# Retention's first rotation behind the value loads, most of y's low parts on GpSimd, and layer 1's low parts one gated block later

## The chip, the cores and the metric

The kernel runs on one core of a Trainium2 chip, as one launch. The metric is the device time of that launch in microseconds (us), lower is better. Five engines work side by side, each through its own list of instructions and in the order of that list: TensorE (PE in the profile: matrix products and transposes, results in banks of PSUM), VectorE (DVE), ScalarE (ACT), GpSimd (POOL) and SyncE (SP), which here does little but start the DMA transfers of the loads and stores. An instruction starts when it is at the head of its engine's list and the semaphores it waits for have come.

## The reference

Two layers on an input of 1024 rows by 1024 columns. Layer 0 projects the normalised input and feeds two branches, an S5 state-space model with a gated linear unit (GLU) and a retention in chunks of 64 rows, each with its gate, and projects both back. Layer 1 is a convolution module. Cut to what the change touches:

```python
# S5 branch, after the scan
y = jax.nn.gelu(y)
y = y * jax.nn.sigmoid(y @ glu_w + glu_b)
# retention: q, k rotated (rope), 8 heads of 64, values 128 wide, 16 chunks of 64 rows
scores = einsum('bnihd,bnjhd->bnhij', qc, kc) * intra
intra_out = einsum('bnhij,bnjhe->bnihe', scores, vc)
kv = einsum('bnjhd,jh,bnjhe->bnhde', kc, k_dec, vc)
_, s_prev = lax.scan(lambda s, kv_n: (chunk_decay * s + kv_n, s), 0, kv)
cross = einsum('bnihd,ih,bnhde->bnihe', qc, q_dec, s_prev)
out = intra_out + cross
out = (out - mean(out)) * rsqrt(var(out) + EPS)          # per head
x = x + concat(y * silu(g_s5), out * silu(g_ret)) @ w_out
# layer 1
a, b, g = split(rmsnorm(x) @ w_in_c, 3)
u = causal_conv31(a * sigmoid(b)) + conv_b
u = silu(layernorm(u)) * silu(g)
x = rmsnorm(x + u @ w_out_c)
```

## The kernel before

**Products.** Everything is held with channels or rows on 128 partitions, in tiles of 128 x 512 (a half of the 1024 rows). To keep float32 accuracy, each operand is split into a high part and a low part: ScalarE casts `f` to `fp32r` (`xh`, `wh`, `yh`), another engine takes the difference (`xl`, `wl`, `yl`), and each block of 128 x 128 x 512 is three matmuls:

```python
nc.tensor.matmul(ps, wh[:, kb, :], xh, start=start, stop=False)
nc.tensor.matmul(ps, wh[:, kb, :], xl, start=False, stop=False)
self.last_mm = nc.tensor.matmul(ps, wl[:, kb, :], xh, start=False, stop=stop)
```

A GLU product is eight such blocks, 24 matmuls, for one half of the rows and 128 columns. Weights come block by block in tiles `wf`, `wh`, `wl` of three buffers each, in the order of a plan (..., V1_0, V1_1, ..., V5_1, k1, q1, k2, ..., glu0, glu1, ...).

**Order.** The program is written as one stream of instructions; a scheduler gives each engine its order by a simulated timeline and by priorities. Inside `with issue_after(x)` an instruction comes no earlier than `x` in that order. The lists that come out are fixed: what stands behind a late instruction on its engine waits with it.

**The values** (`ret_values`). The value projection is made of seven smaller products of sums of blocks (`V_ORDER` 1, 2, 6, 7, 3, 4, 5). `fetch` loads their left operands (`xf30` is block 0 of product 3's operand, here used by product 7), casts (`xh`) and subtracts (`xl`); `scaled` and `summed` add the banks `mm_v` into the value tiles `v`. Between the products `y_pass` loads a part of the S5 output (`yp`), applies gelu on ScalarE and stores it as `yn_d`.

**Retention** works on four pairs of heads. `ret_proj` makes k and q, each times cos and sin (`kcos`, `ksin`), exchanges the sin rows by four DMAs of 128 KB (`kswp<-ksin`), and adds on GpSimd (`krot`, `qrot`). It is a generator; for pair 0 it is run to its end before the values, for the others k's projection comes before the pair ahead and the rest in it. `ret_heads` then runs, per pair: transposes of k (`ktp`, `kt`), `kv`, the 15 state steps `S` one after the other on VectorE, scores `sp` and their mask `sc` (`self.masked`, one per half of the rows), outputs `ro`, statistics (`st`, `mv`, `rs`), normed outputs `on`, transposed back (`rt`) and multiplied into the gate (`grl`).

**Layer 1's low parts.** `weight_low(k)` prepares 32 tiles of layer 1's weights: load `lf`, cast `lh` on ScalarE, subtract, store to DRAM. Tiles 0 to 17 go along with retention's pairs (subtraction on GpSimd), 18 to 31 along with the GLU (on VectorE, two sets of one buffer for each step):

```python
def lows(n):
    for k in islice(left, n):
        self.weight_low(lp, k, (("cs", "pilot"), ("cq", "sq")), 1)
```

**y and the GLU** (`layer0_back_and_layer1`). `load_split` loads y (gelu's output) back in 16 tiles `yf<kb>_<half>`, two to one `wf` buffer, and splits them into `yh`, `yl`. Its order gates, before, are the mask of pair 2 (`self.masked_2`) for the first half, and for the second `self.last_kt` and `self.masked[0]` of pair 3. Each GLU product `mm_glu<nb>_<half>` goes through tanh (`sg`) on ScalarE and `sg = (sg + 1) * yg` on VectorE, where `yg` is the S5 gate times y from GpSimd; for half 0 a split (`ysh`, `ysl`) follows, for half 1 the sums `t3f`, `t2f` that the output projection takes. `lows` is called in both cases.

Of the kernel before, what the change touches and what calls it, by code (L numbers as in the profile page):

```python
# [23 lines left out]
HALF = 512  # L24
# [33 lines left out]
class Trunk:  # L58
# [877 lines left out]
    def retention(self, st):  # L936
        nc, A = self.nc, self.A
        r0 = self.r0 = self.pool("ret0", 1, stack=st)
        early = ExitStack()
        rq = self.rq = self.pool("retq", 1, stack=early, side="right")  # L940
        self.vt = [[(r0 if d else rq).tile([P, 4, HALF], F32, name=f"v{d}_{h}") for h in range(2)] for d in range(2)]
        self.rk = rq.tile([P, 2, T], F32, name="ropek")
        nc.sync.dma_start(self.rk[:], A["rope_k"])
        for i in range(2):
            for c in (slice(0, HALF), slice(HALF, T)):
                nc.gpsimd.tensor_tensor(self.rk[:, i, c], self.rk[:, i, c], self.R[:, c], op=ALU.mult)
        self.mask = r0.tile([P, 4, 64], F32, name="retmask")
        nc.sync.dma_start(self.mask[:], A["ret_mask"])
        self.g64 = r0.tile([P, 4], F32, name="g64")
        nc.sync.dma_start(self.g64[:], A["ret_g64"])  # L950
        self.kdec = r0.tile([P, NH], F32, name="kdec")
        nc.sync.dma_start(self.kdec[:], A["ret_kdec"])
        self.reps = r0.tile([P, NH], F32, name="reteps")
        nc.sync.dma_start(self.reps[:], A["ret_eps"])
        cur = list(self.ret_proj(0))[-1]
        for pair in range(4):
            if pair == 0:
                with ExitStack() as vst:
                    V = self.ret_values(self.pool("vp", 1, stack=vst))
                self.rp = self.pool("ret", 1, stack=st)  # L960
                self.crossed(0)
                ry = self.pool("retl", 1, stack=early, side="right")

            def lows(n, behind):
                with self.tc.issue_after(behind.ins):
                    for k in range(n * LOWS // 6, (n + 1) * LOWS // 6) if pair < 3 else ():
                        self.weight_low(ry, k, (("la", "lb"), ("la", "lb")), 3, nc.gpsimd)

            def turned():
                lows(2 * pair + 1, self.last_kt)  # L970
                if pair == 3:
                    early.close()
                    self.lp = self.pool("l1", side="right")
            lows(2 * pair, self.last_rs if pair else self.last_sum)
            ahead = pair in AHEAD and self.ret_proj(pair + 1)
            if ahead:
                next(ahead)
            cur = self.ret_heads(pair, *cur, V, turned, lambda: list(ahead)[-1] if ahead else None)
            if pair < 3:
                self.crossed(pair + 1)  # L980

    def ret_proj(self, pair):
        nc, A, rp = self.nc, self.A, self.r0
# [14 lines left out]
        def turn(nm):  # L998
            cos, sin = parts[nm]
            swp = self.rq.tile([P, T], F32, name=f"{nm}swp_{pair}", tag="swp", bufs=1)  # L1000
            o = rp.tile([P, T], F32, name=f"{nm}rot_{pair}", tag=f"{nm}rot", bufs=1)
            for b in range(4):
                s = b ^ 1
                nc.sync.dma_start(swp[32 * b:32 * b + 32, :], sin[32 * s:32 * s + 32, :])
            for c in (slice(0, HALF), slice(HALF, T)):
                nc.gpsimd.tensor_tensor(o[:, c], cos[:, c], swp[:, c], op=ALU.add)
            return o


        project("k")  # L1010
        yield None
        krot = turn("k")
        project("q")
        yield krot, turn("q")

    def ret_values(self, vp):
# [4 lines left out]
        def fetch(i, tiles):  # L1021
            for kb, (a, b) in enumerate(tiles):
                g = self.vec(V_NG0, kb)
                f = vp.tile([P, HALF], F32, name=f"xf{i}{kb}", tag="xf", bufs=4)
                nc.sync.dma_start(f[:], self.xt_d[i][kb] if i else self.A["xT"][kb, :, HALF:])
                if i:
                    nc.scalar.copy(a[:], f[:])
                    v.tensor_tensor(b[:], f[:], a[:].bitcast(F32), op=ALU.subtract)
# [177 lines left out]
    def layer0_back_and_layer1(self, st):  # L1206
# [42 lines left out]
        for nb, h in [(nb, h) for nb in range(6) for h in range(2)] + [(6, 0), (7, 0), (6, 1), (7, 1)]:  # L1249
# [12 lines left out]
            if h == 0:  # L1262
                a, b = (self.op_tile(opB, "B0", f"ys{q}{nb}") for q in "hl")
                nc.scalar.mul(a[:], sg[:], 0.5)
                glu_end = v.scalar_tensor_tensor(b[:], sg[:], 0.5, a[:].bitcast(F32), op0=ALU.mult, op1=ALU.subtract)
                ys0[nb], sg0[nb] = (a, b), sg
                lows(2 if nb else 0)
                continue
            yr1 = lp.tile([P, HALF], F32, name=f"yr1_{nb}", tag="tp", bufs=TP)
            nc.sync.dma_start(yr1[:], self.yr_d[rows(nb), hs(1)])  # L1270
            t3f[nb], t2f[nb] = (opB.tile([P, HALF], F32, name=f"{n}_{nb}", tag="B1") for n in ("t3f", "t2f"))
            v.scalar_tensor_tensor(t3f[nb][:], sg[:], -0.5, yr1[:], op0=ALU.mult, op1=ALU.add)
# [508 lines left out]
```

## Time and profile before

| | us |
|---|---|
| median of 3 runs (1184.87, 1189.07, 1189.58) | 1189.07 |
| profiled execution | 1189.67 |
| its span, first to last instruction | 1187.9 |
| busy TensorE | 1159.5 |
| busy VectorE | 906.0 |
| busy GpSimd | 693.9 |
| busy ScalarE | 542.8 |
| mean granted TensorE clock | 0.994 |

A row of a view reads: start and duration in us, engine, line, operation, out<-in by the program's names (with their numbers left out), shapes, how many in a row, and in brackets the idle time of that engine just ahead and what ended it. A row with a bar (|) is a group: busy time in all and mean ns of one, then the idle time before its members. `SPq` is SyncE's queue, busy while a transfer is being issued. `min/median/max` rows are in ns. Line numbers are those of the kernel before.

### The profile page before, as it was taken

How to read it: one execution, taken by the hardware profiler on the slowest of the kernel's cores; microseconds unless marked ns; L12 is line 12 of the kernel's file. 1: busy time of each engine (PE TensorE's matmuls, PEld its weight loads, DVE VectorE, ACT ScalarE, POOL GpSimd, SP SyncE). 2: the span in 40 equal slices, each digit the busy share in tenths (PEclk: the TensorE clock that was granted, in tenths of full speed). 3: DMA queues.
4: the chain of work that ended last, by engine and by line, in shares of the span. 5: the costliest groups of instructions: out<-in, count | busy, mean ns of one | idle time of the engine just before them, and what ended most of it. 6: DMA issues, size and time to landing. Idle time of an engine off the chain costs nothing.

```text
span 1187.9 us, 18547 instructions
## 1 busy us (share of the span) xinstructions
PE 1159.5 (98%) x6662; PEld 962.4 (81%) x6662; DVE 906.0 (76%) x1531; ACT 542.8 (46%) x819; POOL 693.9 (58%) x495
## 2 busy tenths in 40 slices
PE   9999999999999999998899999999999999999997
PEld 7888888888888788886778788778888888888877
DVE  7875789999615577678766887469999999989633
ACT  7212333332226633122543535367755678444662
POOL 2049999888732335452343033428895679977742
PEclk9999999999999999999999999999999999999999
DMA  9353478788888768878986577776448654357863
GB/s 341 107 183 102 140 271 311 267 278 279 268 302 286 254 208 270 231 232 260 348 292 214 156 231 241 271 258 204 169 141 300 231 179 133 121 180 250 271 242 142
DMA packets 135548, 272.17 MB, mean 229 GB/s; under 512 B 13216, under 2 KB 46368, under 8 KB 135328
## 3 DMA queue, kind: packets, MB, share of 16 engines
q1 hardware_dynamic: 134304, 266.80, 67.4%
q10 hardware_dynamic: 1152, 4.19, 0.9%
q8 instruction: 52, 0.85, 0.3%
q14 instruction: 40, 0.33, 0.1%
HBM read 192.89 MB, written 71.76 MB: 223 GB/s over the span
## 4 chain that ended last, share of the span: by engine, by line
PE 82%; DMA 9%; DVE 4%; ACT 1%; POOL 1%; issue 1%; SPq 1%; DVEq 0%; POOLq 0%; ACTq 0%
PE mm_g L277 7%; PE mm_g L278 7%; PE mm_g L276 7%; PE mm_w L278 3%; PE mm_w L276 3%; PE mm_w L277 3%; PE mm_a L278 2%; PE mm_b L277 2%; PE mm_a L277 2%; PE mm_a L276 2%; PE mm_b L278 2%; PE mm_oc L278 2%; PE mm_u L278 2%; PE mm_b L276 2%; PE mm_u L277 2%; PE mm_oc L277 2%
## 5 line engine op out<-in xcount | busy, mean ns | idle before, releaser
L1471 DVE SCALAR_TENSOR_TENSOR cv<-u,convw,cv 128x512 f32<-128x512 f32 x358 | 244.8, 751 | 6.6 <-ACT cv L1457 5.1
L1451 POOL TENSOR_TENSOR tp<-tp,tp 128x512 f32<-128x512 f32 x104 | 138.8, 1337 | 30.7 <-ACT tp L1450 25.4
L278 PE MATMUL mm_g<-xh,wl_g 128*128 128x512 f32 x256 | 100.9, 394 | 0.0
L277 PE MATMUL mm_g<-xl,wh_g 128*128 128x512 f32 x256 | 100.7, 393 | 0.0
L276 PE MATMUL mm_g<-xh,wh_g 128*128 128x512 f32 x256 | 100.6, 393 | 0.0
L1450 ACT ACTIVATE tp<-u,convw 128x512 f32<-128x512 f32 x104 | 69.7, 714 | 11.0 <-POOL tp L1451 10.8
L277 PEld LDWEIGHTS mm_g<-xl,wh_g 128*128 128x128 f32 x256 | 48.1, 188 | 11.2 <-issue 1.6
L278 PEld LDWEIGHTS mm_g<-xh,wl_g 128*128 128x128 f32 x256 | 48.1, 188 | 10.5
L276 PEld LDWEIGHTS mm_g<-xh,wh_g 128*128 128x128 f32 x256 | 48.1, 188 | 9.5
L278 PE MATMUL mm_oc<-zh,wl_woc 128*128 128x512 f32 (+1 forms) x152 | 54.5, 360 | 1.3 <-DMA wl_woc<-lo_woc 1.3
L276 PE MATMUL mm_glu<-yh,wh_glu 128*128 128x512 f32 x128 | 51.1, 399 | 4.6 <-ACT sg L1260 4.1
L276 PE MATMUL mm_oc<-zh,wh_woc 128*128 128x512 f32 (+1 forms) x152 | 54.3, 362 | 0.0
L277 PE MATMUL mm_oc<-zl,wh_woc 128*128 128x512 f32 (+1 forms) x152 | 54.0, 357 | 0.0
L278 PE MATMUL mm_a<-h1h,wl_ca 128*128 128x512 f32 x128 | 50.1, 392 | 1.6 <-DMA wl_ca<-lo_ca 1.6
L277 PE MATMUL mm_u<-xl,wh_u 128*128 128x512 f32 x128 | 50.0, 390 | 0.9 <-DVE xl L390 0.9
L277 PE MATMUL mm_glu<-yl,wh_glu 128*128 128x512 f32 x128 | 50.8, 397 | 0.0
L278 PE MATMUL mm_glu<-yh,wl_glu 128*128 128x512 f32 x128 | 50.5, 394 | 0.0
L276 PE MATMUL mm_g<-h1h,wh_cg 128*128 128x512 f32 x128 | 50.4, 394 | 0.0
L276 PE MATMUL mm_a<-h1h,wh_ca 128*128 128x512 f32 x128 | 50.3, 393 | 0.0
L278 PE MATMUL mm_b<-h1h,wl_cb 128*128 128x512 f32 x128 | 50.3, 393 | 0.0
L278 PE MATMUL mm_g<-h1h,wl_cg 128*128 128x512 f32 x128 | 49.9, 390 | 0.0
L277 PE MATMUL mm_g<-h1l,wh_cg 128*128 128x512 f32 x128 | 49.9, 390 | 0.0
(812 smaller groups left out, 3600.7 us busy)
## 6 DMA issues: line engine op xcount, KB each, us to landing
wf_g<-w_ab SPq DMA_DIRECT2D x16, 512.0 KB, 5.4
a<-w_out SPq DMA_DIRECT2D x32, 256.0 KB, 4.1
ws<-a SPq DMA_DIRECT2D x32, 256.0 KB, 4.7
lf<-w_c SPq DMA_DIRECT2D x32, 256.0 KB, 5.2
wf_p<-ws SPq DMA_DIRECT2D x16, 512.0 KB, 4.1
wf_cb<-w_c SPq DMA_DIRECT2D x16, 512.0 KB, 5.1
wf_ca<-w_c SPq DMA_DIRECT2D x16, 512.0 KB, 4.9
wl_cb<-lo_cb SPq DMA_DIRECT2D x16, 512.0 KB, 3.6
```

The source lines that it names most:

```text
L276: nc.tensor.matmul(ps, wh[:, kb, :], xh, start=start, stop=False)
L277: nc.tensor.matmul(ps, wh[:, kb, :], xl, start=False, stop=False)
L278: self.last_mm = nc.tensor.matmul(ps, wl[:, kb, :], xh, start=False, stop=stop)
L1450: nc.scalar.mul(sk[:], u[:, k:k + HALF], cw[:, nb, k:k + 1])
L1451: gp.tensor_tensor(s0[:], s0[:], sk[:], op=ALU.add)
L1471: v.scalar_tensor_tensor(dst[:], *tap, accs_[i][:], op0=ALU.mult, op1=ALU.add)
```

## The change

Three edits. (1) For pair 0, k and q are projected first, and the exchanges and additions of both come behind the values: the generator is started ahead of `ret_values` and finished after it, and the exchanges carry the gate `issue_after(self.fetched)`, the last load of `fetch`. For the other pairs the gate is that same load, long past. (2) In `load_split`, y's first half and the even tiles of the second go to GpSimd without a gate; the odd tiles of the second stay on VectorE, gated as before. (3) `lows` in the GLU starts one block later in both places: from block 2 on. There are still 14 tiles, and as many matmuls.

```diff
@@ -952,12 +952,14 @@
         nc.sync.dma_start(self.kdec[:], A["ret_kdec"])
         self.reps = r0.tile([P, NH], F32, name="reteps")
         nc.sync.dma_start(self.reps[:], A["ret_eps"])
-        cur = list(self.ret_proj(0))[-1]
+        first = self.ret_proj(0)
+        next(first)
         for pair in range(4):
             if pair == 0:
                 with ExitStack() as vst:
                     V = self.ret_values(self.pool("vp", 1, stack=vst))
                 self.rp = self.pool("ret", 1, stack=st)
+                cur = list(first)[-1]
                 self.crossed(0)
                 ry = self.pool("retl", 1, stack=early, side="right")
 
@@ -999,18 +1001,24 @@
             cos, sin = parts[nm]
             swp = self.rq.tile([P, T], F32, name=f"{nm}swp_{pair}", tag="swp", bufs=1)
             o = rp.tile([P, T], F32, name=f"{nm}rot_{pair}", tag=f"{nm}rot", bufs=1)
-            for b in range(4):
-                s = b ^ 1
-                nc.sync.dma_start(swp[32 * b:32 * b + 32, :], sin[32 * s:32 * s + 32, :])
+            with self.tc.issue_after(self.fetched.ins):
+                for b in range(4):
+                    s = b ^ 1
+                    nc.sync.dma_start(swp[32 * b:32 * b + 32, :], sin[32 * s:32 * s + 32, :])
             for c in (slice(0, HALF), slice(HALF, T)):
                 nc.gpsimd.tensor_tensor(o[:, c], cos[:, c], swp[:, c], op=ALU.add)
             return o
 
 
         project("k")
-        yield None
-        krot = turn("k")
-        project("q")
+        if pair:
+            yield None
+            krot = turn("k")
+            project("q")
+        else:
+            project("q")
+            yield None
+            krot = turn("k")
         yield krot, turn("q")
 
     def ret_values(self, vp):
@@ -1022,7 +1030,7 @@
             for kb, (a, b) in enumerate(tiles):
                 g = self.vec(V_NG0, kb)
                 f = vp.tile([P, HALF], F32, name=f"xf{i}{kb}", tag="xf", bufs=4)
-                nc.sync.dma_start(f[:], self.xt_d[i][kb] if i else self.A["xT"][kb, :, HALF:])
+                self.fetched = nc.sync.dma_start(f[:], self.xt_d[i][kb] if i else self.A["xT"][kb, :, HALF:])
                 if i:
                     nc.scalar.copy(a[:], f[:])
                     v.tensor_tensor(b[:], f[:], a[:].bitcast(F32), op=ALU.subtract)
@@ -1218,7 +1226,12 @@
 
             def put(kb, h, f):
                 a, b = (self.op_tile(self.opA, f"A{h}", f"{name}{q}{kb}_{h}") for q in "hl")
-                self.split(f, a, b, v, None if halves else self.masked_2 if h == 0 else self.last_kt if kb < 6 else self.masked[0])
+                if halves:
+                    self.split(f, a, b, v)
+                elif h == 0 or kb % 2 == 0:
+                    self.split(f, a, b, gp)
+                else:
+                    self.split(f, a, b, v, self.last_kt if kb < 6 else self.masked[0])
                 res[h].append((a, b))
             for h in range(2):
                 for kb in range(KB):
@@ -1264,14 +1277,14 @@
                 nc.scalar.mul(a[:], sg[:], 0.5)
                 glu_end = v.scalar_tensor_tensor(b[:], sg[:], 0.5, a[:].bitcast(F32), op0=ALU.mult, op1=ALU.subtract)
                 ys0[nb], sg0[nb] = (a, b), sg
-                lows(2 if nb else 0)
+                lows(2 if nb > 1 else 0)
                 continue
             yr1 = lp.tile([P, HALF], F32, name=f"yr1_{nb}", tag="tp", bufs=TP)
             nc.sync.dma_start(yr1[:], self.yr_d[rows(nb), hs(1)])
             t3f[nb], t2f[nb] = (opB.tile([P, HALF], F32, name=f"{n}_{nb}", tag="B1") for n in ("t3f", "t2f"))
             v.scalar_tensor_tensor(t3f[nb][:], sg[:], -0.5, yr1[:], op0=ALU.mult, op1=ALU.add)
             glu_end = v.scalar_tensor_tensor(t2f[nb][:], sg0.pop(nb)[:], 0.5, t3f[nb][:], op0=ALU.mult, op1=ALU.add)
-            lows(1 if 0 < nb < 6 else 0)
+            lows(1 if 1 < nb < 6 else 0)
 
         def operand(name, tag, f):
             a, b = (self.op_tile(opB if tag[0] == "B" else self.opA, tag, f"{name}{q}") for q in "hl")
```

What this does to the lists of the engines, at four places. In the rows behind the change the line numbers are those of the changed kernel (3 to 13 higher behind the edits). First SyncE in the middle of the value loads; before:

```order
L159 DMA wf_V6_1_3746<-vs6_1_3147 128x1024
L1004 DMA kswp_0_3523<-ksin_0_3518 32x1024 x4
L1025 DMA xf30_3628<-xt3_1395 128x512
L159 DMA wf_V7_0_3790<-vs7_0_3110 128x1024
L1025 DMA xf31_3632<-xt3_1395 128x512
L931 DMA yp_2_3964<-y_d_83 128x8x128
L1025 DMA xf32_3636<-xt3_1395 128x512
L1025 DMA xf33_3640<-xt3_1395 128x512
L931 DMA yp_6_3969<-y_d_83 128x8x128
L159 DMA wf_V7_1_3820<-vs7_1_3146 128x1024
L1025 DMA xf40_3850<-xt4_1397 128x512
L1004 DMA qswp_0_3593<-qsin_0_3538 32x1024 x4
```

After, the value loads follow one another there, and k's and q's exchanges stand behind the last of them:

```order
L1033 DMA xf02_4108<-xT 128x512
L1033 DMA xf03_4112<-xT 128x512
L1007 DMA kswp_0_4196<-ksin_0_3518 32x1024 x2
L931 DMA yp_3_4026<-y_d_83 128x8x128
L931 DMA yp_7_4031<-y_d_83 128x8x128
L1007 DMA kswp_0_4196<-ksin_0_3518 32x1024 x2
L159 DMA wf_V5_1_4070<-vs5_1_3149 128x1024
L265 DMA wf_k1_4124<-w_ab 128x1024
L265 DMA wf_q1_4154<-w_ab 128x1024
L1007 DMA qswp_0_4204<-qsin_0_3530 32x1024 x4
```

Two yp loads, three weights' loads and the last value loads now stand ahead of the exchanges.

VectorE at the end of value product 6, whose banks are read out into `v` before product 7 goes on adding in them; before, and then after:

```order
L1028 TENSOR_TENSOR xtl3_3611<-xf33_3640,xth3_3610 128x512
L1028 TENSOR_TENSOR xl_0_1_143<-xf40_3850,xh_0_1_142 128x512
L167 TENSOR_TENSOR wl_V7_1_3823<-wf_V7_1_3820,wh_V7_1_3822 128x1024
L1036 TENSOR_SCALAR v0_1_3500<-mm_v1_0_3644,Rtok_368 128x512
L1028 TENSOR_TENSOR xl_1_1_159<-xf41_3854,xh_1_1_158 128x512
```

```order
L1048 SCALAR_TENSOR_TENSOR v0_0_3499<-mm_v2_3_3699,Rtok_368,v0_0_3499 128x512
L1036 TENSOR_TENSOR xl_0_1_143<-xf40_3834,xh_0_1_142 128x512
L1036 TENSOR_TENSOR xl_1_1_159<-xf41_3838,xh_1_1_158 128x512
L1044 TENSOR_SCALAR v0_1_3500<-mm_v1_0_3628,Rtok_368 128x512
L167 TENSOR_TENSOR wl_V7_1_3807<-wf_V7_1_3804,wh_V7_1_3806 128x1024
```

`wl_V7_1` has moved behind the first `v`, and `xl_1_1` ahead of it.

GpSimd ahead of the GLU, between the last low parts of retention's share (`lh_17`), the rotation of pair 3 and the first gates `yg`; before, and then after:

```order
L233 TENSOR_TENSOR lh_17_5233<-lf_17_5232,lh_17_5233 128x512
L268 TENSOR_TENSOR wl_glu1_5473<-wf_glu1_5471,wh_glu1_5472 128x1024
L1006 TENSOR_TENSOR krot_3_5464<-kcos_3_5150,kswp_3_5463 128x512 x2
L1006 TENSOR_TENSOR qrot_3_5534<-qcos_3_5477,qswp_3_5533 128x512 x2
L1256 TENSOR_TENSOR yg0_0_5959<-yg0_0_5959,yn0_0_5961 128x512
L1256 TENSOR_TENSOR yg0_1_5996<-yg0_1_5996,yn0_1_5998 128x512
L1256 TENSOR_TENSOR yg1_0_6041<-yg1_0_6041,yn1_0_6043 128x512
```

```order
L268 TENSOR_TENSOR wl_glu1_5473<-wf_glu1_5471,wh_glu1_5472 128x1024
L1212 TENSOR_TENSOR yl0_0_5868<-yf0_0_5865,yh0_0_5867 128x512
L1212 TENSOR_TENSOR yl1_0_5873<-yf0_0_5865,yh1_0_5872 128x512
L1212 TENSOR_TENSOR yl2_0_5879<-yf2_0_5876,yh2_0_5878 128x512
L1212 TENSOR_TENSOR yl3_0_5884<-yf2_0_5876,yh3_0_5883 128x512
L1212 TENSOR_TENSOR yl4_0_5890<-yf4_0_5887,yh4_0_5889 128x512
L1212 TENSOR_TENSOR yl5_0_5895<-yf4_0_5887,yh5_0_5894 128x512
L1212 TENSOR_TENSOR yl6_0_5901<-yf6_0_5898,yh6_0_5900 128x512
L1212 TENSOR_TENSOR yl7_0_5906<-yf6_0_5898,yh7_0_5905 128x512
L1212 TENSOR_TENSOR yl0_1_5912<-yf0_1_5909,yh0_1_5911 128x512
L1009 TENSOR_TENSOR krot_3_5464<-kcos_3_5150,kswp_3_5463 128x512 x2
L1009 TENSOR_TENSOR qrot_3_5534<-qcos_3_5477,qswp_3_5533 128x512 x2
```

Nine low parts of y now stand between `wl_glu1` and pair 3's rotation. The other side of it is VectorE, at the end of pair 2, behind the second mask (`sc_2`) and around the statistics of heads 4 and 5; before, and then after:

```order
L1132 TENSOR_TENSOR sc_2_5289<-sp1_2_5308,retmask_3509 128x512
L1204 TENSOR_TENSOR yl0_0_5868<-yf0_0_5865,yh0_0_5867 128x512
L1204 TENSOR_TENSOR yl1_0_5873<-yf0_0_5865,yh1_0_5872 128x512
L1204 TENSOR_TENSOR yl2_0_5879<-yf2_0_5876,yh2_0_5878 128x512
L1204 TENSOR_TENSOR yl3_0_5884<-yf2_0_5876,yh3_0_5883 128x512
L1204 TENSOR_TENSOR yl4_0_5890<-yf4_0_5887,yh4_0_5889 128x512
L1204 TENSOR_TENSOR yl5_0_5895<-yf4_0_5887,yh5_0_5894 128x512
L1167 BN_STATS st_4_0_5362<-ro0_4_5330 128x6 x4
L1167 BN_STATS st_5_0_5375<-ro0_5_5331 128x6 x4
L1204 TENSOR_TENSOR yl6_0_5901<-yf6_0_5898,yh6_0_5900 128x512
L1168 BN_AGGR mv_4_0_5363<-st_4_0_5362 128x2 x4
L1204 TENSOR_TENSOR yl7_0_5906<-yf6_0_5898,yh7_0_5905 128x512
```

```order
L1140 TENSOR_TENSOR sc_2_5289<-sp1_2_5308,retmask_3509 128x512
L1175 BN_STATS st_4_0_5362<-ro0_4_5330 128x6 x4
L1175 BN_STATS st_5_0_5375<-ro0_5_5331 128x6 x2
L1176 BN_AGGR mv_4_0_5363<-st_4_0_5362 128x2
L1175 BN_STATS st_5_0_5375<-ro0_5_5331 128x6
L1176 BN_AGGR mv_4_0_5363<-st_4_0_5362 128x2
L1175 BN_STATS st_5_0_5375<-ro0_5_5331 128x6
L1176 BN_AGGR mv_4_0_5363<-st_4_0_5362 128x2 x2
L1176 BN_AGGR mv_5_0_5376<-st_5_0_5375 128x2 x4
```

The eight low parts of y's first half are gone from there, and the statistics follow the mask.

Last, VectorE in the GLU, around `t3f_0`; before, and then after:

```order
L1186 TENSOR_TENSOR grl_6_5682<-rt1_6_5836,grl_6_5682 128x512
L1261 SCALAR_TENSOR_TENSOR sg2_0_6172<-sg2_0_6172,yg2_0_6142 128x512
L1186 TENSOR_TENSOR grl_7_5684<-rt1_7_5842,grl_7_5684 128x512
L233 TENSOR_TENSOR lh_26_6334<-lf_26_6333,lh_26_6334 128x512
L233 TENSOR_TENSOR lh_27_6383<-lf_27_6382,lh_27_6383 128x512
L1272 SCALAR_TENSOR_TENSOR t3f_0_6031<-sg0_1_6026,yr1_0_6029 128x512
L1265 SCALAR_TENSOR_TENSOR ysl0_5993<-sg0_0_5989,ysh0_5992 128x512
L1273 SCALAR_TENSOR_TENSOR t2f_0_6032<-sg0_0_5989,t3f_0_6031 128x512
```

```order
L233 TENSOR_TENSOR lh_22_6269<-lf_22_6268,lh_22_6269 128x512
L1194 TENSOR_TENSOR grl_7_5684<-rt1_7_5842,grl_7_5684 128x512
L1274 SCALAR_TENSOR_TENSOR sg2_0_6153<-sg2_0_6153,yg2_0_6123 128x512
L233 TENSOR_TENSOR lh_23_6314<-lf_23_6313,lh_23_6314 128x512
L233 TENSOR_TENSOR lh_24_6363<-lf_24_6362,lh_24_6363 128x512
L1285 SCALAR_TENSOR_TENSOR t3f_0_6031<-sg0_1_6026,yr1_0_6029 128x512
L1278 SCALAR_TENSOR_TENSOR ysl0_5993<-sg0_0_5989,ysh0_5992 128x512
L1286 SCALAR_TENSOR_TENSOR t2f_0_6032<-sg0_0_5989,t3f_0_6031 128x512
```

`t3f_0` stood behind low part 27 and now stands behind low part 24.

## The prediction

> **What bounds the kernel now.** I read the page's totals first, then the list of who waited for whom on TensorE, then the busy time and clock by stage.
>
> ```profile
> span 1187.9 us, 18547 instructions
> PE 1159.5 (98%) x6662; PEld 962.4 (81%) x6662; DVE 906.0 (76%) x1531; ACT 542.8 (46%) x819; POOL 693.9 (58%) x495
> ```
>
> TensorE (PE) is idle for 28.4 us of 1187.9. No matmul is added or removed, so the change can win only idle time, or time at a low clock.
>
> ```profile
> PE mm_glu L276 <- ACT sg L1260: 4.1, 2, 2.8
> PE mm_v L1058 <- DVE v L1036: 2.9, 1, 2.9
> PE rt L1183 <- DVE mv L1168: 2.8, 1, 2.8
> PE sp L1129 <- DVE S L1121: 2.0, 1, 2.0
> PE kv L1113 <- DVE kt L1101: 0.9, 1, 0.9
> PE mm_glu L276 <- DVE qcos L996: 0.5, 1, 0.5
> ```
>
> Total, times and longest, in us. These are all of TensorE's waits in the stages that the change touches (values, retention's last pairs, GLU): 13.2 us together.
>
> ```profile
> 395.00:400.00 5.00, 5.00 (x16) 3.95 (x16) 5.00 (x6) 2.80 (x5) 4.06 (x3) 0.66 0.79 270
> 545.00:550.00 5.00, 4.50 (x19) 3.53 (x18) 5.00 (x15) 4.74 (x8) 0.00 (x0) 0.66 0.59 148
> 565.00:570.00 5.00, 4.93 (x110) 4.55 (x114) 4.78 (x12) 2.28 (x3) 0.00 (x0) 0.66 1.05 404
> 580.00:585.00 5.00, 3.78 (x21) 3.22 (x22) 5.00 (x24) 4.36 (x8) 1.59 (x1) 1.00 0.78 272
> ```
>
> Busy time by stretch; the last three columns are granted clock, DMA share and GB/s. Behind three of the waits (mm_v, rt, sp) five microseconds ran at 0.66, which costs 0.34 x 5 = 1.7 us each; behind the 2.8 us wait for sg the clock stayed at 1.00. So 13.2 + 5.1 = 18.3 us can be won at most, 1.5% of the time.
>
> [...]
>
> **Part 1, the exchange of pair 0's rows.** Eight transfers leave the middle of the value loads.
>
> ```profile
> 368.62 2.96 SPq L1004 DMA_DIRECT2D kswp<-ksin  x4
> 383.74 2.67 SPq L1004 DMA_DIRECT2D qswp<-qsin  x4
> qswp<-qsin SPq DMA_DIRECT2D x4, 128.0 KB, 7.2
> 393.43 0.62 ACT L1027 CAST xh<-xf 128x512 fp32r<-128x512 f32 x1 [0.72 <-DMA xf<-xt]
> 391.80 0.69 DVE L1028 TENSOR_TENSOR xl<-xf,xh 128x512 fp32r<-128x512 f32 x1 [1.92 <-ACT xh L1027]
> 392.74 1.23 DVE L167 TENSOR_TENSOR wl_V<-wf_V,wh_V 128x1024 fp32r<-128x1024 f32 x1 [0.25 <-ACT wh_V L166]
> 393.88 0.74 DVE L1036 TENSOR_SCALAR v<-mm_v,Rtok 128x512 f32<-128x512 f32 x1
> 394.78 0.47 PE L1058 MATMUL mm_v<-wh_V,xth 128*128 128x512 f32 x1 [2.87 <-DVE v L1036]
> ```
>
> SyncE's queue first, then ScalarE, VectorE and TensorE. Product 7 was free to start at 394.78 - 2.87 = 391.91. It waits for v at 393.88, a result whose matmuls are done, but which stands in VectorE's order behind xl (its load landed at 391) and wl_V. In the new order v stands behind two xl, xf40's and xf41's, and ahead of wl_V; xf41's cast is the one at 393.43. What moves it up: the exchanges took 2.96 + 2.67 = 5.6 us of issue ahead of it, and their 1 MB, in a stretch that moves some 361 GB/s, 2.9 us of transfer.
>
> ```profile
> 390.00:395.00 5.00, 2.13 (x10) 1.50 (x9) 2.95 (x4) 2.18 (x3) 1.86 (x1) 1.00 1.03 361
> ```
>
> With 2.9 us: 393.43 - 2.9 + 0.62 + 0.69 + 0.74 = 392.6, so a wait of 0.7 us is left; with 5.6 us none. Gain 2.2 to 2.9 us, and the 1.7 of clock: I take 4.2, between 0 (another load becomes the late one) and 4.6.
>
> What the exchanges now stand behind: all fetches, two yp loads and wf_q1, which waits until GpSimd is done with wl_V5_0. On GpSimd, krot and qrot now stand ahead of wl_k1.
>
> ```profile
> 423.96 2.40 POOL L167 TENSOR_TENSOR wl_V<-wf_V,wh_V 128x1024 fp32r<-128x1024 f32 x1 [6.82 <-ACT wh_V L166]
> 377.00 3.66 POOL L1006 TENSOR_TENSOR krot<-kcos,kswp 128x512 f32<-128x512 f32 x2 [15.80 <-DMA kswp<-ksin]
> 431.10 2.51 POOL L268 TENSOR_TENSOR wl_k<-wf_k,wh_k 128x1024 fp32r<-128x1024 f32 x1 [4.74 <-ACT wh_k L267]
> 440.54 1.04 PE L1099 MATMUL ktp<-ident,krot 128*128 128x128 f32 x8
> ```
>
> wl_V5_0 ends at 426.36 at the latest; q's exchanges issue by 429.4 and land 7.2 us after their issue, so by 434 to 436.6; qrot takes 3.66 and wl_k1 2.51, so wl_k1 is there between 440 and 442.8. TensorE wants krot at 440.54 and wl_k1 at about 441.8, both 4.2 earlier if the gain is made. But wl_V5_0 hangs on TensorE's progress and moves up with it, and in the new order its cast on ScalarE comes ahead of a 2 us gelu. So I count nothing here, with 0 to 3 us of loss as the bound.
>
> **Part 2, y's low parts.** Twelve of 16 subtractions go from VectorE to GpSimd, the first eight without their gate.
>
> ```profile
> L1204 DVE TENSOR_TENSOR yl<-yf,yh 128x512 fp32r<-128x512 f32 x8 | 7.2, 950 | 0.0
> L1006 POOL TENSOR_TENSOR krot<-kcos,kswp 128x512 f32<-128x512 f32 x2 | 3.4, 1728 | 7.1 <-DVE yl L1204 7.1
> L1204 DVE TENSOR_TENSOR yl<-yf,yh x16: 654/684/1776, 530.7 to 568.6; 128x512 fp32r<-128x512 f32 x16
> L233 POOL TENSOR_TENSOR lh<-lf,lh x18: 1277/1293/1302, 447.2 to 520.6; 128x512 fp32r<-128x512 f32 x18
> 531.75 1.26 ACT L1202 CAST yh<-yf 128x512 fp32r<-128x512 f32 x2 [8.15 <-DMA yf<-yn_d]
> 544.51 1.06 PE L1183 MATMUL rt<-ident,on 128*128 128x128 f32 x8 [2.84 <-DVE mv L1168]
> ```
>
> Groups of 528 to 546 us, then minimum, median and maximum of one. VectorE spends 7.2 us on eight yl ahead of and between the statistics of pair 2, and rt waits for those: without them on_5_0 (done at 544.4) comes near 537. TensorE needs it, in the new order, after 11 of GLU's matmuls, about 538.3 plus nothing. The 2.84, the 0.50 for qcos (same queue) and the clock's 1.7 go: 5.0 us. The same low parts on GpSimd: four at 1.29 us before yf4's cast at 531.75, five behind it: 532.4 + 5 x 1.29 = 538.8. TensorE takes yl4 to yl7 from 538.6 to 542 and yl0_1 near 543, so they are in time by 3 us or more; krot of pair 3 follows at 538.8 + 2.6 = 541.4 where it is wanted near 546.
>
> ```profile
> 556.53 4.16 DVE L1204 TENSOR_TENSOR yl<-yf,yh 128x512 fp32r<-128x512 f32 x5
> 562.63 2.63 DVE L1121 SCALAR_TENSOR_TENSOR S<-S,g,kv 128x128 f32<-128x128 f32 x7
> ```
>
> In pair 3 the state steps S (0.38 us each) start behind six yl and two lh; now behind three yl and no lh. That takes away kt's 0.9, S's 2.0 and its 1.7 of clock: 4.6 us. What is late next: the outputs of the second half need 15 steps, two masks and one yl, some 7 to 8 us behind kv, and TensorE has 5.6 to 6.5 us of other work there (sp, 11 GLU matmuls at 0.23, the first half's outputs). I charge 1.5 us, bounds 0 and 3.7 (2.0 and another 1.7 of clock). Part 2: 5.0 + 4.6 - 1.5 = 8.1 us.
>
> **Part 3, layer 1's low parts one block later.** VectorE works in order, and a low part whose load has not landed holds up all behind it.
>
> ```profile
> L233 DVE TENSOR_TENSOR lh<-lf,lh 128x512 fp32r<-128x512 f32 x14 | 10.9, 781 | 15.5 <-ACT lh L232 15.5
> 553.33 0.90 SPq L231 DMA_DIRECT2D lf<-w_c  x2
> 575.82 0.69 DVE L233 TENSOR_TENSOR lh<-lf,lh 128x512 fp32r<-128x512 f32 x1 [3.95 <-ACT lh L232]
> 618.38 0.63 ACT L232 CAST lh<-lf 128x512 fp32r<-128x512 f32 x1 [1.61 <-DMA lf<-w_c]
> 605.91 0.69 ACT L1260 ACTIVATE sg<-mm_glu,hgb 128x512 f32<-128x512 f32 x1 [1.86 <-DVE t3f L1272]
> 606.65 0.50 PE L276 MATMUL mm_glu<-yh,wh_glu 128*128 128x512 f32 x1 [1.29 <-ACT sg L1260]
> ```
>
> 15.5 us of VectorE's idle time stand before the 14 lh. lh_20 at 575.82 stood inside pair 3's statistics, and behind them the 2.81 us wait for sg; lh_18 and lh_19 now stand there, whose loads issue, by SyncE's new order (behind wf_glu3, yn2_0 and grl_7), only some 2 us later than at 553.33 though TensorE is 9 us earlier. So part of that wait stays: I take a gain of 1.5, between 0 and 2.8. At 606.65 TensorE waits for a bank whose sg waits for t3f_0, which stands behind lh_27 and will stand behind lh_24. The chain of low parts has two buffers a step and runs at its own pace, 553.33 to 618.38 for seven rounds of two, 9.3 us a round. Starting 2 us later it reaches lh_24 one and a half rounds before its old lh_27, 12 us earlier: t3f_0 10 us earlier against TensorE's 9.5. The 1.29 stays, and from here the chain, not TensorE, may set the pace: I give back 2 us, between 0 and 4.
>
> **Sum.** 4.2 + 8.1 + 1.5 - 2.0 = 11.8 us. The profiled execution took 1189.67 us (span 1187.9), 0.6 over the median of 1189.07; 1189.07 - 11.8 = 1177.3, say 1177. Behind the GLU nothing is changed, and TensorE is the busiest engine up to the first convolution block, so I let the shift carry through.
>
> **Rivals.** (a) GpSimd's subtractions slow VectorE's. For it: yl took up to 1.776 us instead of 0.684 while krot ran, and krot 1.728 instead of 1.293. If the three yl and sg0_0 ahead of S each lose 1.1 us, S starts 4.4 us later, the sp wait and its clock come back, and the gain is 4.2 + 5.0 - 4.4 = 4.8: 1184. Against it: most of VectorE's work there reads PSUM, and pair 2's ran beside GpSimd's lh undisturbed. [...]
>
> (b) The waits move, and nothing is won behind the values: lf_18 slips not 2 but 8 us, because y's and the gates' loads go first, and TensorE meets t3f_0 at its old distance. Gain 4.2, or 2 to 3 if a late wl_k1 costs some of it: 1186. For it: 1.05 of DMA at 404 GB/s from 565 to 570. Against it: 0.59 at 545 to 550.
>
> (c) Slower: the low parts' chain stretches. sg5_0 stands behind lh_31 on ScalarE in the new order, and the product two blocks on (near 634 now) needs its bank. If a round took over 12.5 us instead of 9.3, lh_31 came 22 us later, past 640, and the kernel ended 6 us or more later, 1196. Against it: loads landed in at most 7.4 us.
>
> ```profile
> DMA to landing us min/median/max: 2.7/5.2/7.4
> ```
>
> **How the numbers follow.** A measurement of this kernel can tell about 0.5%, 5.9 us, from no change. Forecast, gain 7 to 17: 0.55. All waits gone, under 1172: 0.06. (a), 1182 to 1186: 0.20, of which 0.08 below 1183.1. (b): 0.13. (c): 0.06. Faster by over 0.5%: 0.55 + 0.06 + 0.08 = 0.69; within: 0.12 + 0.12 = 0.24; slower: 0.07. The range runs from all 18.3 us won (1171) to (a) and half of (b), 1187.
>
> **What would show it.** Part 1: no wait of mm_v for v near 391, clock 1.00 there, krot's first rotation ending before ktp. Part 2: no wait of rt for mv, yl on GpSimd at 1.3 us, S starting within 1 us of kv. Part 3: VectorE's idle time before lh well under 15.5 us, and t3f_0 near 594 on this profile's clock, less part 1. Wrong if a new wait of over 3 us stands at wl_k, ro or mm_glu, or the convolution's start does not move up with the GLU's end.

## The result and the profile after

The changed kernel takes 1176.33 us (median of 4 runs, 1174.54 to 1176.60), the kernel before 1189.32 in the same comparison: ratio 0.9896, 95% interval 0.9871 to 0.9922, that is 12.4 us less (9 to 15; the medians alone differ by 13.0). Forecast were 1177 and a gain of 11.8. The profiled execution took 1176.18 us. Of all executions behind this document two, one of the kernel before (1289.58 us) and one of the run set3_only (1942.62), ran at a much lower clock (0.849 and 0.556) and are left out of the ratios.

The totals of the page, after:

```profile
span 1174.4 us, 18560 instructions
PE 1154.8 (98%) x6662; PEld 958.0 (82%) x6662; DVE 901.2 (77%) x1519; ACT 543.2 (46%) x819; POOL 707.3 (60%) x507
```

TensorE is idle for 19.6 us (28.4 before) and busy for 4.7 us less with the same 6662 matmuls. Most of that is the clock: before, three stretches of 3.41 us ran at 0.50, which is 5.1 us of lost work; after, none did until the last 2 us. From the list of who waited for whom on TensorE, after (total, times, longest):

```profile
PE mm_w L278 <- DVE wl_p L167: 3.1, 2, 2.3
PE rt L1191 <- DVE on L1185: 1.7, 1, 1.7
PE mm_w L276 <- ACT sg L1273: 1.6, 1, 1.6
PE ro L1162 <- issue: 0.8, 1, 0.8
PE sp L1137 <- DVE S L1129: 0.8, 1, 0.8
PE ro L1162 <- DVE S L1129: 0.5, 1, 0.5
```

Gone are the waits for v (2.9), for mv (2.8), kt (0.9) and qcos (0.5) and both of mm_glu for sg (4.1); the one of sp for S fell from 2.0 to 0.8. New are one of rt for on (1.7), one of the output projection's first matmul for sg (1.6), and a wait for wl_p that grew from 1.4 to 2.3. Busy time by stretch (the clock is the third column from the end):

```profile
395.00:400.00 5.00, 5.00 (x23) 4.02 (x23) 2.43 (x3) 2.70 (x5) 0.60 (x1) 1.00 0.56 209
535.00:540.00 5.00, 5.00 (x27) 4.17 (x26) 5.00 (x24) 3.30 (x6) 1.11 (x1) 1.00 0.83 192
555.00:560.00 5.00, 4.27 (x120) 3.42 (x115) 3.48 (x9) 1.62 (x2) 2.44 (x2) 1.00 1.03 404
565.00:570.00 5.00, 3.34 (x20) 2.64 (x19) 4.86 (x25) 4.34 (x7) 2.35 (x1) 1.00 1.02 374
```

The clock is 1.00 behind the values, at the end of pair 2 and in pair 3 (some 9 us earlier now), the three places where it was 0.66.

**Part 1's place**, after: ScalarE, three of VectorE, then the groups of pair 0's first transposes (min/median/max in ns, then first and last start) of after and of before.

```profile
387.53 1.28 ACT L1035 CAST xh<-xf 128x512 fp32r<-128x512 f32 x2 [2.18 <-DMA xf<-xt]
388.18 1.35 DVE L1036 TENSOR_TENSOR xl<-xf,xh 128x512 fp32r<-128x512 f32 x2 [2.24 <-ACT xh L1035]
389.45 0.74 DVE L1044 TENSOR_SCALAR v<-mm_v,Rtok 128x512 f32<-128x512 f32 x1
390.12 1.22 DVE L167 TENSOR_TENSOR wl_V<-wf_V,wh_V 128x1024 fp32r<-128x1024 f32 x1
L1107 PE MATMUL ktp<-ident,krot x32: 271/273/273, 435.7 to 542.3; 128*128 128x128 f32 x32
L1099 PE MATMUL ktp<-ident,krot x32: 272/273/273, 440.5 to 554.7; 128*128 128x128 f32 x32
```

The second cast starts at 388.2 (393.43 before) and v at 389.45 (393.88 before), ahead of wl_V; no wait is left. TensorE leaves the values 4.8 us earlier (435.7 against 440.5).

**Part 2's place**, after: y's low parts on both engines, VectorE in pair 3, and the sp matmuls.

```profile
L1212 POOL TENSOR_TENSOR yl<-yf,yh x12: 1267/1287/1720, 518.1 to 553.6; 128x512 fp32r<-128x512 f32 x12
L1212 DVE TENSOR_TENSOR yl<-yf,yh x4: 692/1299/1759, 543.9 to 555.6; 128x512 fp32r<-128x512 f32 x4
547.84 3.44 DVE L1212 TENSOR_TENSOR yl<-yf,yh 128x512 fp32r<-128x512 f32 x2
551.20 0.28 DVE L1127 COPY S<-kv 128x128 f32<-128x128 f32 x1
553.99 0.97 PE L1137 MATMUL sp<-qrot,krot 64*64 64x64 f32 x26 [0.84 <-DVE S L1129]
```

GpSimd takes the 1.29 us that was counted. Two of VectorE's four low parts take 1.76 us each instead of 0.69, and sg0_0 ahead of them 1.75 instead of 0.68, beside two low parts and a gate on GpSimd (546.08 to 550.73). S starts behind them.

**Part 3 and the GLU's end**, after: the loads of low parts 18 and 19 and the first t3f; TensorE's last matmul of the product that sg5_0 takes, some of ScalarE in the order of its list, SyncE's last loads yr0f, and the output projection's first waits.

```profile
553.15 1.38 SPq L231 DMA_DIRECT2D lf<-w_c  x2
590.50 0.68 DVE L1285 SCALAR_TENSOR_TENSOR t3f<-sg,yr 128x512 f32<-128x512 f32 x1
608.94 0.39 PE L278 MATMUL mm_glu<-yh,wl_glu 128*128 128x512 f32 x1
618.97 0.62 ACT L232 CAST lh<-lf 128x512 fp32r<-128x512 f32 x1 [3.22 <-DMA lf<-w_c]
619.50 0.68 ACT L1273 ACTIVATE sg<-mm_glu,hgb 128x512 f32<-128x512 f32 x1
630.41 6.45 SPq L1296 DMA_DIRECT2D yr0f<-yr_d  x4
635.17 0.62 ACT L1210 CAST yr03h<-yr0f 128x512 fp32r<-128x512 f32 x1 [5.19 <-DMA yr0f<-yr_d]
637.75 0.68 ACT L1273 ACTIVATE sg<-mm_glu,hgb 128x512 f32<-128x512 f32 x1
638.48 0.50 PE L276 MATMUL mm_w<-ysh,wh_p 128*128 128x512 f32 x1 [1.64 <-ACT sg L1273]
647.00 0.50 PE L278 MATMUL mm_w<-ysh,wl_p 128*128 128x512 f32 x1 [2.33 <-DVE wl_p L167]
```

The product is done at 609.3; sg5_0 starts at 619.50, because the cast of low part 31 stands ahead of it and waits for its load. The output projection's first matmul then waits for sg7_0 at 637.75. Shortly ahead of that one in ScalarE's list stands a second late load: the cast yr03h waits 5.19 us for yr0f (4.74 before). That sg5_0's delay is what brings it late is not seen link by link here; the run set3 below moves both. Before, sg5_0 waited for nothing but its product:

```profile
623.37 0.69 ACT L1260 ACTIVATE sg<-mm_glu,hgb 128x512 f32<-128x512 f32 x1 [0.45 <-PE mm_glu L278]
```

### The profile page after: what moved, and what is told of

The parts are those of the page before. It is cut to its first block, busy times and chain, and to the rows that moved or that the text cites. A ratio compares the mean times of both kernels' runs of the same rounds, so it can differ in the third digit from the quotient of the medians.

```text
span 1174.4 us, 18560 instructions
## 1 busy us (share of the span) xinstructions
PE 1154.8 (98%) x6662; PEld 958.0 (82%) x6662; DVE 901.2 (77%) x1519; ACT 543.2 (46%) x819; POOL 707.3 (60%) x507
## 5 line engine op out<-in xcount | busy, mean ns | idle before, releaser
L277 PE MATMUL mm_b<-h1l,wh_cb 128*128 128x512 f32 x128 | 49.8, 389 | 0.0
```

## The experiments

All ratios are to the kernel before; 0.001 is 1.2 us.

| kernel | what it has | median, us | ratio, 95% interval |
|---|---|---|---|
| before_again | nothing changed | 1188.30 | 0.9995 [0.9986, 1.0004] |
| p1 | part 1 | 1183.88 | 0.9961 [0.9947, 0.9975] |
| p12 | parts 1, 2 | 1180.99 | 0.9927 [0.9912, 0.9943] |
| p13 | parts 1, 3 | 1184.80 | 0.9969 [0.9957, 0.9982] |
| p23 | parts 2, 3 | 1182.48 | 0.9949 [0.9933, 0.9965] |
| after | all | 1176.33 | 0.9896 [0.9871, 0.9922] |
| dve_nogate | all, y's low parts on VectorE | 1178.58 | 0.9915 [0.9898, 0.9932] |
| yl16 | all, all of them on GpSimd | 1179.36 | 0.9939 [0.9926, 0.9953] |
| set3 | all, third buffer set | 1171.86 | 0.9855 [0.9842, 0.9868] |
| late | all, low parts behind the statistics | 1172.96 | 0.9874 [0.9851, 0.9897] |
| set3_late | both | 1169.02 | 0.9834 [0.9816, 0.9852] |
| set3_t3f | both, and behind t2f_0 | 1168.35 | 0.9836 [0.9824, 0.9849] |
| set3_only | before, third buffer set | 1188.70 | 1.0007 [0.9995, 1.0019] |

**The kernel before again** (no edit): what its executions differ in.

> The kernel before, once more, to see what its executions differ in. [...] Rival: the executions differ by their transfers, with one clock of 0.994 in all.

The profiled execution (1187.58 us), whose trace the last section calls the second profile, has a mean clock of 0.994, as the first profile at 1189.67, where three stretches of 3.41 us ran at 0.50 (the expectations below call one such stretch a window); what it is faster by lies behind the GLU (waits of 0.94, 1.63 and 1.31 us for s1q, wl_ca and wl_woc there; here only one of 0.55, for wl_woc). The eleven executions have mean clocks of 0.992 to 0.995, the fastest (1185.86) 0.995 and the slowest (1191.44) 0.992, but the one of 1188.38 has 0.995 too. So the spread from 1184 to 1191 isn't told by the clock alone, and the rival's single clock is not there either.

**Parts one by one.** p1 and p12 have the first part and the first two, p13 and p23 leave one part out. The edits are against the changed kernel; p23 is the kernel before with the edits of parts 2 and 3.

```diff
-                lows(2 if nb > 1 else 0)          # p12; p1 besides with the old split
+                lows(2 if nb else 0)
-            lows(1 if 1 < nb < 6 else 0)
+            lows(1 if 0 < nb < 6 else 0)
```

> Part 1 alone. Theory: the wait of 2.9 us for v and the half window behind it go, nothing else moves: 4.7 us by the shift of TensorE's matmuls between the two traces (4.88 at the end of the values less 0.17 from the start), so 1184.5, within the 1.7 us that one window of clock is worth. Rival: TensorE arrives 4.7 us early at waits that hang on loads (pair 2's and pair 3's), which grow by what was won: 1187 to 1189.

1183.88: the theory's time, 4.6 us by the ratio (3.0 to 6.3). TensorE's shift at pair 0's first transpose is 4.65 us, and 4.58 are the wait and its clock. That nothing else moves is not so: rt's wait is 3.83 (2.84 before), and the mean clock is 0.995 (0.994 before), from which I estimate some three stretches at half clock, as many as before, though the wait for v is gone.

> Parts 1 and 2, without part 3. Theory: part 2 is worth 6 to 7 us net of the new small waits and part 3 nothing, since what it wins in pair 3 and at the fifth GLU product (2.4 us) is given back where the output projection starts (1.64 and 0.96 us): 1176.5 to 1178. Rival: part 3 is worth its 2.5 us and more, because lh_18 and lh_19 stand among the state steps again and bring back the wait of sp for S (2 us) and its clock (1.7): 1179 to 1181.

1180.99: the rival's size, but not by its mechanism. In p12's waits sp is gone, and rt stands in its place; on VectorE low part 20 holds up the statistics of pair 3. The trace is of the fastest of six executions (1177.24, within the theory's range), so what the others lost besides is not seen:

```profile
PE rt L1191 <- DVE on L1185: 3.8, 1, 3.8
565.07 0.69 DVE L233 TENSOR_TENSOR lh<-lf,lh 128x512 fp32r<-128x512 f32 x1 [4.28 <-ACT lh L232]
```

```diff
                 # p13: the old split
-                if halves:
...
-                    self.split(f, a, b, v, self.last_kt if kb < 6 else self.masked[0])
+                self.split(f, a, b, v, None if halves else self.masked_2 if h == 0 else self.last_kt if kb < 6 else self.masked[0])
```

> Parts 1 and 3 without part 2. Theory (by the waits): rt 2.8, qcos 0.5, kt 0.9 and S 2.0 come back, with one or two windows of clock of 1.7: 1182 to 1186. Rival (part 2 is worth only what it was worth without part 3, 2.9 us): 1179.

1184.80: the theory. In the trace, which is of the slowest of twelve executions (1189.11), rt waits 2.8 us for mv, and sp:

```profile
561.71 1.55 PE L1137 MATMUL sp<-qrot,krot 64*64 64x64 f32 x24 [4.14 <-DVE S L1129]
```

Against p1 (1183.88), part 3 without part 2 gains nothing: low part 18 stands ahead of S here, behind the low parts of y, and VectorE waits 1.53 us for its cast.

> Parts 2 and 3 without part 1 (k's and q's exchanges for pair 0 again among the value loads). Theory: part 1 is worth the same 4.6 us here as alone, since nothing behind the values hangs on loads that it moved: 1181 to 1182, with a wait of 2.5 to 3.8 us of mm_v for v near 392 in the profile. Rival (what is won at the values is partly taken back by later waits in the full change, so that taking it away costs less): 1178 to 1179.

1182.48: the theory, half a us past its range; part 1 is worth 0.0053 in the full change (6 us) and 0.0039 alone (4.6), alike within the intervals. The wait for v is back, without a stretch at half clock behind it (1.00 from 393.95 to 400.78):

```profile
395.21 0.47 PE L1058 MATMUL mm_v<-wh_V,xth 128*128 128x512 f32 x1 [2.78 <-DVE v L1036]
```

**Part 2, engine or gate.**

```diff
-                if halves:
-                    self.split(f, a, b, v)
-                elif h == 0 or kb % 2 == 0:
-                    self.split(f, a, b, gp)
-                else:
-                    self.split(f, a, b, v, self.last_kt if kb < 6 else self.masked[0])
+                self.split(f, a, b, v, None if halves or h == 0 or kb % 2 == 0 else self.last_kt if kb < 6 else self.masked[0])
```

> The changed kernel with all of y's low parts on VectorE; the first half and the even tiles of the second without a gate. In the order they stand among pair 2's state steps, five of them ahead of pair 3's state steps, and low parts 18 and 19 inside those. Theory (the engine matters in pair 3, the gate in pair 2): rt's and kt's waits stay away, but sp waits about 2 us for S again, with a window of clock when it falls so, and 1 to 2 us come where pair 2's S steps are held up: 1179 to 1182. Rival (only the gate mattered): 1176.

1178.58, a little under the theory's range. sp does wait for S, but in pair 2 (531.02), where the ungated low parts now stand among the state steps; in pair 3 mm_glu waits 4.2 us for sg:

```profile
PE sp L1137 <- DVE S L1129: 4.9, 1, 4.9
```

The median is 2.3 us over the changed kernel's, and the intervals overlap. So the waits say that twelve low parts without a gate don't fit on VectorE; whether the engine matters to the time is not settled.

```diff
-                elif h == 0 or kb % 2 == 0:
-                    self.split(f, a, b, gp)
                 else:
-                    self.split(f, a, b, v, self.last_kt if kb < 6 else self.masked[0])
+                    self.split(f, a, b, gp)
```

> The changed kernel with all sixteen low parts of y on GpSimd. Theory of contention (the prediction's first rival in small): in the changed kernel pair 3's state steps start behind two yl of 1.7 us each that run beside GpSimd's, and the waits of sp and ro for S (0.84 and 0.46 us) follow from it; without yl on VectorE they go: 1174.5 to 1175.5. Rival (GpSimd's list becomes the late one): qrot of pair 3 and the first gates now stand behind five more yl and wl_glu2, some 8 us later, and sp waits for qrot instead: 1177 to 1180.

1179.36: slower, though not for qrot (ready at 549.1). GpSimd's first gate waits for its load yn, sg on VectorE waits for the gate, and S waits behind sg, which besides takes 2.82 us beside GpSimd. GpSimd, VectorE, TensorE:

```profile
553.56 1.29 POOL L1267 TENSOR_TENSOR yg<-yg,yn 128x512 f32<-128x512 f32 x1 [4.46 <-DMA yn<-yn_d]
554.88 2.82 DVE L1272 SCALAR_TENSOR_TENSOR sg<-sg,yg 128x512 f32<-128x512 f32 x1 [10.35 <-POOL yg L1267]
561.11 1.66 PE L1137 MATMUL sp<-qrot,krot 64*64 64x64 f32 x26 [5.75 <-DVE S L1129]
```

So whether the slower yl on VectorE cost anything in the changed kernel stays open: this run has another wait in their place.

**The end of the GLU: who sets the pace.**

```diff
-        f = pool.tile([P, HALF], F32, name=f"lf_{k}", tag=tags[k % 2][0], bufs=bufs)
-        hi = pool.tile([P, HALF], F32R, name=f"lh_{k}", tag=tags[k % 2][1], bufs=bufs)
+        f = pool.tile([P, HALF], F32, name=f"lf_{k}", tag=tags[k % len(tags)][0], bufs=bufs)
+        hi = pool.tile([P, HALF], F32R, name=f"lh_{k}", tag=tags[k % len(tags)][1], bufs=bufs)
...
-                self.weight_low(lp, k, (("cs", "pilot"), ("cq", "sq")), 1)
+                self.weight_low(lp, k, (("cs", "pilot"), ("cq", "sq"), ("dg", "sacc")), 1)
```

> The changed kernel with a third set of buffers for layer 1's low parts in the GLU stage. Theory: at the GLU's end the low parts' chain sets the pace (sg5_0 stands behind the cast of low part 31 on ScalarE, done 10 us after its product), so with three tiles under way the wait of the output projection's first matmul for sg (1.64 us) and 1 us of the wait for wl_p go: 1173 to 1174. Rival: it is the loads of yr0 and the gates on SyncE's queue that are late, and they stay where they are or come later: 1176 to 1177.

1171.86, 4.5 us under the changed kernel, intervals apart. Low part 31 is cast at 603.3 instead of 619.0, sg5_0 again follows its product, and the last four loads yr0f start 6.3 us earlier than in the changed kernel:

```profile
609.78 0.69 ACT L1273 ACTIVATE sg<-mm_glu,hgb 128x512 f32<-128x512 f32 x1 [0.47 <-PE mm_glu L278]
624.08 6.28 SPq L1296 DMA_DIRECT2D yr0f<-yr_d  x4
```

Both waits at the output projection's start (1.64, 2.33) and the 0.82 that followed are gone from the list. Whether the third set is worth as much without the change, the same edit on the kernel before tells:

> The kernel before with nothing changed but the third set of buffers for the low parts of the GLU stage. Theory (the chain of low parts became the bound only because TensorE comes earlier in the changed kernel): before, sg5_0 starts 0.1 us after its product is done, so there is nothing to win there but a part of the two waits for wl_p (1.4 and 0.8 us), and two more low parts stand among pair 3's statistics: 1187 to 1189. Rival (the third set is worth its 4.5 us by itself): 1184.

1188.70, ratio 1.0007: nothing on the whole. It is a sum of two things, though: the waits for wl_p (2.2 us) go here too, while more low parts come among pair 3's state steps and statistics, mm_glu's waits for sg grow from 4.1 to 5.7 us, and the mean clock is 0.991 (0.994 before), from which I estimate some five stretches of 3.41 us at half clock instead of three. That sg5_0 was not held up before is shown by its row above, not by this time.

```diff
-        self.nc.scalar.copy(hi[:], f[:])
-        (e or self.nc.vector).tensor_tensor(hi[:], f[:], hi[:].bitcast(F32), op=ALU.subtract)
+        with nullcontext() if e else self.tc.issue_after(self.last_rs.ins):
+            self.nc.scalar.copy(hi[:], f[:])
+            (e or self.nc.vector).tensor_tensor(hi[:], f[:], hi[:].bitcast(F32), op=ALU.subtract)
```

> The same later place of the cast and the subtraction, but with the two sets of buffers of the changed kernel. Theory (the chain of low parts sets the pace at the GLU's end): rt's wait of 1.7 us goes, low part 31 comes later than before by more than that, and the waits at the output projection's start grow from 4.8 us by about the same: 1176 to 1179. Rival (the places among the statistics are what costs): 1174.5.

1172.96 in the median, with executions from 1170 to 1177 and an interval that overlaps the changed kernel's. By the trace the theory fell. The chain did end later (low part 31 cast at 623.0), but it now stands behind sg5_0 in ScalarE's list, sg5_0 starts at 616.27 instead of 619.50, and the waits at the output projection's start shrink from 4.8 to 2.8 us. What counted here is where the low part stands, not when the chain ends.

> The third set of buffers, and in the GLU stage the cast and the subtraction of a low part come behind pair 3's last statistics (the loads stay where they are). Theory: the wait of 1.9 us that is left at 567 (a GLU product for sg0_1, which on ScalarE follows the roots of statistics that stand on VectorE behind low parts 18 to 20 and their loads) goes, and with three tiles under way the chain is still done ahead of sg5_0: 1169.5 to 1170.5. Rival: the chain starts 6 us later and ends later, and the waits for sg and wl_p at the output projection's start come back: 1173 to 1176.

1169.02: a little better than the theory. The wait at 567 is gone, but a new one of 3.1 us comes at 590, where t3f_0 stands behind low part 25. With that moved:

```diff
+        with nullcontext() if e else self.tc.issue_after((self.last_rs if k < 24 else self.first_t2f).ins):
...
+            if nb == 0:
+                self.first_t2f = glu_end
```

> The third set with the low parts behind the statistics, and low parts 24 and on also behind t2f_0: on VectorE, t3f_0 now stands ahead of low parts 24 and 25. Theory: the wait of 3.1 us at 590 (a GLU product for a bank whose sg2_1 waits for t3f_0, which stood behind low part 25 and its load) shrinks to under 1 us, and the window of clock behind it goes where it was: 1166 to 1167.5. Rival (t3f_0 waits for the retention's last store anyway, not for its place): 1169.

The profile does what was meant (no wait for sg is left; the longest of TensorE's waits is 1.1 us, at the kernel's start), but the time, 1168.35 or 0.9836, is that of set3_late within the intervals, a little over the theory's range. Both beat the kernel before by 1.6% and the changed kernel by 7 to 8 us.

## Why the prediction was right, and where only its sum was

**Part 1** was forecast at 4.2 and is 4.7 by the shift in the trace, 4.6 by p1. The 4.7 is the 4.88 us between the first transposes less 0.17 us by which the traces differ ahead of the values. Of the two prices, the 5.6 us of issue time was the near one, not the 2.9 of transfer: the cast of the second load moved by 5.2 us. What the exchanges now stand behind cost nothing, as counted: krot ends at 422.6 and wl_k1 at 432.7, both before TensorE leaves the values.

**Part 2** was forecast at 8.1. Leaving it out costs 0.0073, 8.7 us (p13), but on top of part 1 alone it brings 0.0034, 4.0 us (p12). The step that is not part 2's own is the one that has the state steps "behind three yl and no lh": that there is no low part among and close behind them is part 3's doing. In p12, without part 3, rt waits 3.8 us behind low part 20. So some 4.6 us seem to come only with both parts; from the four intervals I estimate this to 4 us either way, just clear of noise. Together they bring 0.0065 (p1 against after), 7.7 us, where the sum had 8.1 + 1.5 - 2.0 = 7.6. In pair 2 the 2.84 and 0.50 went as forecast, and a wait of 0.84 us of ro came that the trace puts down to nothing; it stays open. In pair 3, "what is late next" was charged with 1.5 and measured 0.84 for S, 0.15 for the mask, 0.46 for S again and 0.32 put down to nothing: 1.8. S did not start within 1 us of kv, as was to be seen: kv begins at 547.54 and S at 551.20.

**Part 3's** 1.5 and the 2.0 given back were mis-sized in their pieces, not in their sum, -0.5. The wait of 2.81 of mm_glu behind pair 3's statistics became one of 1.66 of rt (1.15 won). The 1.29 was said to stay and went: the loads of low parts 18 and 19 were to start 2 us later than at 553.33 and started at 553.15, and t3f_0 comes 13.5 us earlier (604.0 to 590.5), not 10. VectorE's idle time before the low parts fell from 15.5 to 11.1 us; and the chain "may set the pace" held, as set3 against set3_only shows, at 1.64 and 0.96 us. 1.15 + 1.29 - 2.60 = -0.2. Rounds took 9.35 us (loads of low parts 18 to 30: 553.1 to 609.2, six rounds), as counted, so rival (c) never came near, and rival (b) was not there.

**Rival (a)** came in by its condition and not by its price. Of the four instructions ahead of S that were to lose 1.1 us each, three lost 1.07 (sg0_0 and two low parts) and the fourth 0.15: 3.4 us of 4.4. But TensorE had eleven GLU matmuls to do meanwhile, until 553.15, and waited the 1.8 us above, without a stretch at half clock (1.00 from 546 to 556).

**The step that the shift carries through** behind the GLU held only on the whole. TensorE is 11.8 us earlier at the output projection's first matmul (650.3 to 638.5), 10.7 behind the wait for wl_p (657.73 to 647.00) and 13.5 at the end. Of the 2.8 us in between, 2.4 come from the waits for s1q, wl_ca and wl_woc (0.94, 1.63, 1.31 before; 0, 0.95, 0.51 after), which differ among executions of the kernel before as well. So the closeness to 1177 is partly luck.

**The clock**, 5.1 us in the sum, came in full in the profiled execution, but the prediction had no reason why one wait of 2.8 us kept its clock and another of 2.0 lost it, and what decides it was not shown. The new wait of 2.33 us had 1.83 in one stretch of 3.41 us and 1.00 behind it, the old one of 1.96 for S had all of it in one and 0.50 behind it (last section); with so little between them, this too is partly luck.

## What to carry to other kernels

Look for what stands behind a late instruction in an in-order list before moving work to another engine: here the wins were places in a list (v ahead of wl_V, low parts away from the state steps and the statistics), and the clearest loss too (sg5_0 behind a cast that waits for a load). When two edits clear the same stretch, price them together and test them by leaving one out as well as by adding one. After a gain, ask which chain with few buffers keeps its own pace: here it held up no GLU product while TensorE came some 10 us later, and with the change one more buffer set was worth a third of the gain.

## What the chip showed that was not expected: which idle time had half clock behind it

In the first profile of before the clock was 0.50 for 3.41 us from 395.43, 545.62 and 566.10, and from 1183.91 to the end of the span. These four starts lie 150.19, 20.48 and 617.81 us apart, which is 44, 6 and 181 times 3.413 us. In the profile after it was 0.50 only from 1172.16 to the end. I therefore divide the traces into steps of 3.413 us that meet these starts. The rows are stretches of one step each (length, TensorE's busy time, ..., clock, DMA share, GB/s), the first six of before, the next three of its second profile, the last two of after:

```profile
392.02:395.43 3.41, 0.65 (x3) 0.60 (x4) 3.16 (x4) 1.32 (x3) 2.29 (x2) 1.00 1.02 383
395.43:398.84 3.41, 3.41 (x10) 2.67 (x9) 3.41 (x6) 2.17 (x3) 2.47 (x2) 0.50 0.82 282
562.69:566.10 3.41, 1.45 (x42) 1.11 (x44) 3.20 (x10) 0.00 (x0) 1.26 (x1) 1.00 1.05 405
566.10:569.51 3.41, 3.41 (x65) 3.04 (x56) 3.19 (x10) 1.80 (x3) 0.00 (x0) 0.50 1.06 408
579.75:583.16 3.41, 1.94 (x8) 1.56 (x9) 3.41 (x21) 2.78 (x5) 1.84 (x1) 1.00 0.85 291
583.16:586.58 3.42, 3.42 (x21) 2.94 (x20) 3.17 (x9) 3.39 (x6) 0.27 (x1) 1.00 0.74 217
561.34:564.75 3.41, 3.37 (x15) 2.44 (x13) 3.38 (x8) 0.61 (x2) 0.04 (x1) 1.00 1.03 408
564.75:568.16 3.41, 1.47 (x54) 1.50 (x57) 3.20 (x9) 0.27 (x1) 1.23 (x1) 1.00 1.06 408
568.16:571.57 3.41, 2.17 (x62) 1.68 (x57) 3.22 (x9) 1.97 (x3) 0.00 (x0) 1.00 1.04 400
643.09:646.50 3.41, 1.58 (x7) 0.96 (x6) 2.69 (x4) 3.41 (x6) 1.30 (x1) 1.00 0.22 77
646.50:649.91 3.41, 2.91 (x13) 2.42 (x14) 3.41 (x7) 0.72 (x2) 0.00 (x0) 1.00 0.54 153
```

Idle 2.76 and 1.96 us in one step: the next step ran at 0.50. The wait of 2.81 us at 578.41 falls on two steps, 1.34 and 1.47: the next ran at 1.00. The second profile has 1.94 in one step (564.75): the next ran at 1.00. The wait of 2.33 in the changed kernel has 1.83: the next ran at 1.00. From 10 us on, before has four steps with more than 1.83 us idle (2.76, 2.36, 1.96, and 2.15 ahead of the last start) and after has one (3.41, ahead of its only start); 0.50 followed each of these five and no other step of the two traces. Of the three half steps of before, two had no idle time and one 0.46 us, and 1.00 followed each; in dve_nogate one with 2.54 (528.48) and in yl16 one with 3.13 (557.98) were followed by a second. So before, the waits of 2.87 for v and 1.96 for S were each followed by 3.41 us at half clock, 1.7 us more, and the one of 2.81 for sg cost only itself. In p23 the wait of 2.78 for v has 1.52 and 1.26 in its two steps and costs only itself. What makes the clock fall these rows do not show.
